# Two output-column blocks of the first branch's gates: five pairs of k-tiles instead of four by seven products, all four weight sums read from DRAM

## The chip, the cores and the metric

One core of a Trainium2 chip runs the whole program. The metric is device time in microseconds (us), the median of several executions. Three executions of the kernel before took 1547.37, 1547.99 and 1548.03 us, so the median is 1547.99 us. A profiled execution of the same kernel is what all rows below come from; its own time was 1548.36 us.

## The reference

The program is one layer of a decoder trunk for 256 positions of width 2048, all in float32:

```python
h = rms_norm(x, norm_mix_pre[l]);  proj = h @ w_in[l]
a_in, b_in, q, kv, nsa_g, merge_g = jnp.split(proj, splits, axis=-1)
y_a, y_b, y_c = conformer_conv(a_in, ...), chunked_spatial_gating(b_in, ...), native_sparse_attention(q, kv, nsa_g, ...)
g_a, g_b, g_c = jnp.split(jax.nn.sigmoid(merge_g), 3, axis=-1)
x = x + rms_norm((g_a * y_a + g_b * y_b + g_c * y_c) @ w_o[l], norm_mix_post[l])
h = rms_norm(x, norm_ffn_pre[l]);  u = causal_dwconv3(h @ w_up[l]);  u_g, u_v = jnp.split(u, 2, axis=-1)
x = x + rms_norm((silu(u_g) * u_v) @ w_down[l], norm_ffn_post[l])
```

The change touches the product `h @ w_in` for `merge_g`, and in it the 2048 columns of `g_A`, the gates of the first branch.

## The kernel before

**Products.** TensorE works on float32 values that are split in two: a high part of fewer bits (`hi`, copied by ScalarE) and the rest (`lo`, subtracted by VectorE). One product of a 128x128 tile by 128x512 weights is three matmuls: high by high, high by rest, rest by high. Each block of weights thus goes through a load into one of five buffers `wraw` (queued on SyncE, "SP" in the profile), a copy on ScalarE (ACT) into one of four buffers `whi`, and a subtraction on VectorE (DVE) into one of four buffers `wlo`.

**Sevens.** A gate block is 256 positions by 1024 columns, over 16 k-tiles. Two halves of positions by two halves of columns by two k-tiles are a 2x2 by 2x2 product of blocks: eight block products, 24 matmuls, when done plainly (`k_tiles`), or seven, 21 matmuls, by Winograd's form of Strassen's method (`Seven.seven`). The seven need four sums of weight blocks and some sums of activations (`sh`, `s3`, made for five pairs while attention runs, in `input_sums`). Seven's products go to four main accumulators `c` and four side accumulators `p1`, `p5`, `p6`, `p7`; `combine` adds the sides up at the end, and `totals` adds the main ones and takes the tanh. In a `seven`, SP loads the blocks `b` and half of `r` from the weights, and sums from DRAM: `a` (two sums, into one of two buffers `qa`), one more into the other half of `r`, and, if four sums are in DRAM, the fourth into `tt`. If only three are there, VectorE adds the fourth into `tt` itself. ScalarE and VectorE then split `b`, `a`, `r` and `t` (a half block).

**The sums in DRAM.** GpSimd (POOL) issues DMAs that build the weight sums in DRAM tiles `ahead`, long before they are used: a copy of blocks, then DMAs that add other blocks to them. `ahead_steps` yields these steps in a fixed order: gate blocks 0 to 3, the output projection ("o"), then the 33 pairs of the down projection. `ahead_by(mark, n)` issues the next `n` of them when a given result of the main work exists: POOL first copies one column of it into `tick`, which makes it wait. POOL runs in order, one DMA after the other, each waiting for those that it adds to. Steps that are left at the end of the first half are spread over the 44 iterations of the up projection.

**Order of the work.** First the projections of the branches, the convolution and the attention's inputs; then `branch()` (gates and output of the second branch, column block `cb` 0 to 3) and `outs_a()` (output of the first) with attention in between as background work; then the gate blocks `gates_7(0)` and `gates_7(1)` (first branch), `gates_7(2)` and `gates_7(3)` (third branch, with its output projection), the output projection "o", the up projection, the down projection in two column halves ("pair 0" and "pair 1"). Gate block `i` begins with `lead` plain k-tiles, then come `len(GP[i])` sevens with `between[j]` plain tiles ahead of seven `j`, then the remaining plain tiles. `then()` is emitted after the lead tiles: for block 0 it lets attention finish, for block 1 it takes the totals of block 0 and multiplies the gates into the sum (`gate_a`). Matmuls of these blocks are chained in the order in which they are written (`in_line`), so are the splits on ACT and DVE (`fixed`); the rest is ordered by a scheduler. Names in the rows: `g03b` is block `b` of gate block 0, seven 3; `pg` main, `pg0s` side accumulators; `Ct<-O` the last step of attention.

Of the kernel before, what the change touches and what calls it, by code (L numbers as in the profile page):

```python
# [23 lines left out]
F32 = mybir.dt.float32  # L24
# [10 lines left out]
NFT = FF // 128  # L35
# [8 lines left out]
NEXT = ((6, 4, 5, 0), (1, 2))  # L44
SUMS = [[2 + (n % 2 or n >= 16) for n in range(len(TURNS[0]))], [3 + (n % 2 == 0) for n in range(len(TURNS[1]))]]

GP = [[0, 1, 2, 3]] * 3 + [[0, 1, 2, 3, 4]]
GREST = [list(range(2 * len(gp), KT)) for gp in GP]
OP, OREST = [0, 1, 2, 4], [6, 7, *range(10, KT)]
BA, BB, BC, BG, RUSH, SUMS_AT = 2100, 2200, 2200, 6500, 1.0, 3  # L50
PR = 1000
# [14 lines left out]
def block(ctx: ExitStack, tc: tile.TileContext, x, xf, x0, fp, cst, rows, sgw, w1, w2, wf_a, wt_bv, wf_bu, wf_c,  # L66
# [58 lines left out]
    def pooled(op, *args, **kw):  # L125

        with ExitStack() as order:
            for ins in in_pool:
                order.enter_context(tc.issue_after(ins))
            in_pool[:] = [op(*args, **kw).ins]  # L130

    tick = PZ.tile([128, 1], F32, name="tick")
    made = {}

    def ahead_steps():

        quads = [(("g", cp, j), (wt_gq[cp, j] if cp < 3 else wt_cq[j]), 3) for cp in range(4) for j in range(len(GP[cp]))]
        quads += [(("o", j), wt_oq[j], 3) for j in range(len(OP))]
        quads += [((p, j), (wt_dq0, wt_dq1)[p][n], SUMS[p][n]) for p in range(2) for n, j in enumerate(TURNS[p])]
        add = {"accum_op": ALU.add}  # L140
        late = []
        for i, (key, src, sums) in enumerate(quads):
            dst = DR.tile([128, sums, 512], F32, name=f"ahead{i}")
            made[key] = dst, sums
            src = src.rearrange("p (b n) -> p b n", b=4)
            yield dst[:, 0:2], src[:, 2:4], {}
            if late:
                yield late.pop(0)
            if sums > 2:
                yield dst[:, 2:], src[:, 4 - sums:2], {}  # L150
            yield from late
            yield dst[:, 0:2], src[:, 1:3], add
            late = [(dst[:, x], dst[:, y], add) for x, y in ((sums - 1, 1), (2, 3))[:sums - 2]]
        yield from late

    steps = list(ahead_steps())

    def ahead_by(mark, n):

        pooled(G.tensor_copy, tick, mark)  # L160
        for dst, src, how in steps[:n]:
            pooled(G.dma_start, dst, src, **how)
        del steps[:n]

    def split2(raw):
# [1027 lines left out]
    def branch():  # L1193

        for cb in range(4):
            pg = [PS.tile([128, 512], F32, tag="acc", name=f"pg0{cb}{t}") for t in range(2)]
            for q in range(4):
                hs = granule(wt_g[cb * 4 + q])
                for k, ts_ in in_order(q):
                    hi, lo = hs[(k % 4) // 2]  # L1200
                    c = slice((k % 2) * 512, (k % 2) * 512 + 512)
                    for t in ts_:
                        ts = slice(t * 128, t * 128 + 128)
                        with ExitStack() as order:
                            if (cb, k) == (1, 0):
                                order.enter_context(tc.issue_after(norm["v"]))
                            mm_t(pg[t], hT[:, k, 0, ts], hT[:, k, 1, ts], hi[:, c], lo[:, c], k == 0, k == KT - 1)
                if (cb, q) == (0, 2):
                    until("m")
                    debt[0] = 0.0  # L1210
                elif q < 3:
                    if (cb, q) == (1, 2):
                        marks.add("outputs")
                    pump(BUDGET)
            tgs = {}
            for t in range(2):
                for a in range(2):
                    tgs[t, a] = q1(f"mg0{cb}{t}{a}")
                    with tc.high_priority(offset=int(PR)):
                        gated[0] = S.activation(tgs[t, a], pg[t][:, a * 256:a * 256 + 256], AF.Tanh,  # L1220
                                                scale=rh[:, t:t + 1]).ins
            marks.add("gates")
            pump(BUDGET)
            py = [PS.tile([128, 512], F32, tag="acc", name=f"py0{cb}{t}") for t in range(2)]
            for q in range(2):
                hs = granule(wt_p[cb * 2 + q])
                if cb == 0 and q == 0:
                    until("B")
                act = Bt_box["t"]
                for k, ts_ in in_order(q):  # L1230
                    hi, lo = hs[(k % 4) // 2]
                    c = slice((k % 2) * 512, (k % 2) * 512 + 512)
                    for t in ts_:
                        ts = slice(t * 128, t * 128 + 128)
                        with ExitStack() as order:
                            if (cb, k) == (0, 7):
                                until("v")
                                debt[0] = max(debt[0], 0.0)
                                order.enter_context(tc.issue_after(norm["v"]))
                            pe_last[0] = mm_t(py[t], act[:, k, 0, ts], act[:, k, 1, ts], hi[:, c], lo[:, c], k == 0, k == 7)  # L1240
                if q == 0:
                    pump(BUDGET)
            for t in range(2):
                for a in range(2):
                    cc = slice(cb * 512 + a * 256, cb * 512 + a * 256 + 256)
                    y = mac[:, t, cc]
                    with tc.high_priority(offset=int(PR)):
                        V.scalar_tensor_tensor(y, tgs[t, a], 1.0, py[t][:, a * 256:a * 256 + 256], op0=ALU.add,
                                               op1=ALU.mult)
            ahead_by(mac[:, 0, cb * 512:cb * 512 + 1], (4, 8, 12, 8)[cb])  # L1250
            pump(BUDGET)

    def outs_a():

        for cb in range(4):
# [14 lines left out]
                with tc.high_priority(offset=int(PR)):  # L1270
                    V.tensor_copy(ya[:, t, cb * 512:cb * 512 + 512], py[t])
            if cb < 3:
                ahead_by(ya[:, 0, cb * 512:cb * 512 + 1], (8, 4, 0)[cb])
            pump(BUDGET)

    def m_sums(n):
# [69 lines left out]
    def gates_7(i, between, lead=2, then=None):  # L1346
# [4 lines left out]
        def begin():  # L1351
            if then:
                then()
            pr.p1, pr.p5, pr.p6, pr.p7 = four(i, "s")
            gates_of.append(s8([128, 2, 2, 512], F32, f"gates{i}"))
        in_sevens(pr, wt_gp[i] if i < 3 else wt_cp, wt_gq[i] if i < 3 else wt_cq, GREST[i], between, hx, g_acts, ("g", i), lambda j: box["qa"][:, j % 2],
                  lambda: box["tt"], f"g{i}", lead, begin)
        return pr

# [11 lines left out]
        return then  # L1371

    prs = []
    prs.append(gates_7(0, (0, 0, 0, 0), 6, attended))
    prs.append(gates_7(1, (1, 0, 0, 0), 4, gated_a(0)))
    for cp in range(2):
        pr = gates_7(2 + cp, (0,0,0,0,0) if cp else (1,0,0,0), 3 if cp else 4, None if cp else gated_a(1))
        gates = gates_of[2 + cp]
# [271 lines left out]
    for i in range(NFT):  # L1650
# [19 lines left out]
        for j, (k0, k1) in enumerate(PAIRS):  # L1670
            if i == k0:
                first = acc[0]
            elif i == k1:
# [8 lines left out]
                    pooled(G.dma_start, extra[j], apart_.bitcast(F32))  # L1682
                if j < AWAY:
                    pooled(G.dma_start, away[j], dst.rearrange("p x a b -> p x (a b)").bitcast(F32))
        ahead_by(g2(i, slice(0, 1))[0].bitcast(F32), max(0, len(steps) - count * (NFT - 2 - i) // (NFT - 2)))
    P2b_ctx.close()


# [235 lines left out]
def _layout(inp):  # L1924
# [92 lines left out]
                c(np.concatenate([w[k1, 0], w[k1, 1], w[k0, 1], w[k0, 0]], axis=2)))  # L2017

    sevens = [by_sevens(w_in[:, g_cols[2048 + 1024 * i:3072 + 1024 * i]], GP[i], GREST[i]) for i in range(4)]
    wt_gp, wt_gq = (np.stack(a) for a in zip(*sevens[:3]))  # L2020
    wt_cp, wt_cq = sevens[3]
    wt_op, wt_oq = by_sevens(g["w_o"][0][:, 0:1024], OP, OREST)

    xf = c(g["x"].reshape(T, KT, 128).transpose(2, 1, 0))
# [26 lines left out]
```

## Time and profile before

| | |
|---|---|
| median of the timed runs | 1547.99 us (1547.37 to 1548.03) |
| the profiled execution, its own time | 1548.36 us |
| span from its first to its last instruction | 1546.7 us |
| TensorE busy | 1538.8 us, 99% of the span |
| VectorE, ScalarE, GpSimd busy | 86%, 62%, 15% |
| granted TensorE clock | 1.00 throughout |
| gate blocks of the first branch | 528 us (first matmul of block 0) to 613 us (end of block 1) |

In a row of a group of instructions, the count is followed by the busy time and the mean duration of one, and then by the idle time of the engine just before them and what ended it. Durations of matmuls overlap, since they are pipelined: the pace is read from a run of matmuls without a break in the chain of waits (time of the run over their number). A timeline row has start, duration, engine, line, operation, tiles and, in brackets, the idle time before it. A windows row gives for one stretch the busy time of each engine, the granted clock, the mean busy share of the 16 DMA engines and the bytes moved. "SPq" is the queue of DMAs on SyncE.

### The profile page before, as it was taken

How to read it: one execution, taken by the hardware profiler on the slowest of the kernel's cores; microseconds unless marked ns; L12 is line 12 of the kernel's file. 1: busy time of each engine (PE TensorE's matmuls, PEld its weight loads, DVE VectorE, ACT ScalarE, POOL GpSimd, SP SyncE). 2: the span in 40 equal slices, each digit the busy share in tenths (PEclk: the TensorE clock that was granted, in tenths of full speed). 3: DMA queues.
4: the chain of work that ended last, by engine and by line, in shares of the span. 5: the costliest groups of instructions: out<-in, count | busy, mean ns of one | idle time of the engine just before them, and what ended most of it. 6: DMA issues, size and time to landing. Idle time of an engine off the chain costs nothing.

```text
span 1546.7 us, 23457 instructions
## 1 busy us (share of the span) xinstructions
PE 1538.8 (99%) x8138; PEld 1313.3 (85%) x8138; DVE 1336.8 (86%) x2282; ACT 961.5 (62%) x1509; POOL 229.8 (15%) x350
## 2 busy tenths in 40 slices
PE   9999999999999999999999999999999999999998
PEld 8888889888877788888888888888888888888887
DVE  7899999978778689979878888888888888899898
ACT  7645544456776766656666666666565656576774
POOL 1021460211121100000000122222222221100000
PEclk9999999999999999999999999999999999999999
DMA  9598997998889877767884699999999999989895
GB/s 372 189 299 266 293 295 224 271 289 270 251 243 266 257 241 267 254 221 262 270 268 160 207 307 332 316 324 295 292 280 288 279 292 285 324 283 344 315 380 207
DMA packets 131512, 428.24 MB, mean 277 GB/s; under 512 B 15104, under 2 KB 16880, under 8 KB 130624
## 3 DMA queue, kind: packets, MB, share of 16 engines
q1 hardware_dynamic: 99936, 329.99, 60.8%
q0 software_dynamic: 30880, 96.09, 26.2%
q8 instruction: 64, 1.05, 0.3%
q10 hardware_dynamic: 576, 0.66, 0.1%
q14 instruction: 56, 0.46, 0.1%
HBM read 418.55 MB, written 92.01 MB: 330 GB/s over the span
## 4 chain that ended last, share of the span: by engine, by line
PE 95%; issue 2%; DVE 2%; DMA 1%; ACT 0%; POOL 0%; DVEq 0%; POOLq 0%
PE ps L229 29%; PE ps L236 15%; PE pg L1096 8%; PE pd1a L1096 4%; PE pd0b L1096 4%; PE pd0a L1096 3%; PE pd1b L1096 3%; PE py L250 3%; PE py L251 3%; PE py L252 3%; PE poa L1096 2%; PE pg L251 1%; PE pg L252 1%; PE pg L250 1%; PE po L252 1%
## 5 line engine op out<-in xcount | busy, mean ns | idle before, releaser
L200 ACT ACTIVATE whi<-wraw 128x1024 fp32r<-128x1024 f32 (+1 forms) x344 | 361.1, 1055 | 205.5 <-PE ps L229 115.0
L201 DVE TENSOR_TENSOR wlo<-wraw,whi 128x1024 fp32r<-128x1024 f32 (+1 forms) x344 | 419.1, 1224 | 72.7 <-ACT whi L200 54.1
L229 PE MATMUL ps<-h2T,whi 128*128 128x512 f32 x1360 | 317.2, 390 | 0.0
L229 PEld LDWEIGHTS ps<-h2T,whi 128*128 128x128 f32 x1360 | 252.4, 188 | 50.4
L236 PEld LDWEIGHTS ps<-h2T,wlo 128*128 128x128 f32 x1360 | 169.4, 192 | 3.6
L236 PE MATMUL ps<-h2T,wlo 128*128 128x256 f32 x1360 | 170.7, 283 | 0.0
L229 PE MATMUL ps<-hT,whi 128*128 128x512 f32 x640 | 151.7, 390 | 0.0
L229 PEld LDWEIGHTS ps<-hT,whi 128*128 128x128 f32 x640 | 118.0, 188 | 23.0
L1052 DVE TENSOR_TENSOR wlowraw<-wraw,whiwraw 128x1024 fp32r<-128x1024 f32 x72 | 87.1, 1222 | 25.7 <-ACT whiwraw L1052 23.6
L558 DVE SCALAR_TENSOR_TENSOR cv<-hb,fps,cv 128x256 f32<-128x256 f32 x240 | 107.0, 502 | 0.1
L1052 ACT ACTIVATE whiwraw<-wraw 128x1024 fp32r<-128x1024 f32 x72 | 75.6, 1057 | 38.6 <-PE py L252 10.1
L1660 ACT ACTIVATE fa<-fs,fps 128x256 f32<-128x256 f32 x88 | 52.7, 598 | 53.6 <-DVE fs L275 51.7
L236 PEld LDWEIGHTS ps<-hT,wlo 128*128 128x128 f32 x640 | 80.8, 191 | 2.6 <-DVE wlo L201 0.3
L236 PE MATMUL ps<-hT,wlo 128*128 128x256 f32 x640 | 82.3, 283 | 0.1
L130 POOL DMA_DIRECT2D ahead<-ahead x54 | 44.3, 821 | 241.8 <-DMA ahead<-in_wt_dq_dram 104.0
L130 POOL DMA_DIRECT2D ahead<-in_wt_dq_dram x91 | 69.4, 879 | 71.5 <-DMA ahead<-in_wt_dq_dram 70.4
L272 ACT ACTIVATE t<-ps 128x256 f32<-128x256 f32 x125 | 47.5, 381 | 49.5 <-PE ps L236 26.5
L1096 PE MATMUL pg<-whiwraw,hT 128*128 128x512 f32 x240 | 75.5, 390 | 0.0
L130 POOL COPY tick<-gh 128x1 f32<-128x1 f32 x44 | 35.1, 799 | 192.0 <-ACT gh L1668 192.0
L1661 DVE SCALAR_TENSOR_TENSOR fa<-fs,fps,fa 128x255 f32<-128x255 f32 x88 | 42.4, 481 | 16.6 <-ACT fa L1660 16.5
L1096 PEld LDWEIGHTS pg<-whiwraw,hT 128*128 128x128 f32 x240 | 45.0, 188 | 10.1 <-issue 0.8
L273 DVE TENSOR_TENSOR t<-ps,t 128x256 f32<-128x256 f32 x125 | 52.7, 424 | 0.5 <-ACT t L272 0.5
(2568 smaller groups left out, 3345.8 us busy)
## 6 DMA issues: line engine op xcount, KB each, us to landing
wraw<-in_wf_up_dram SPq DMA_DIRECT2D x176, 512.0 KB, 6.9
ahead<-in_wt_dq_dram POOLq DMA_DIRECT2D x74, 512.0 KB, 10.1
wraw<-in_wt_p_dram SPq DMA_DIRECT2D x48, 512.0 KB, 6.4
wraw<-in_wt_dq_dram SPq DMA_DIRECT2D x33, 512.0 KB, 5.7
wraw<-in_wf_a_dram SPq DMA_DIRECT2D x32, 512.0 KB, 5.6
wraw<-in_wt_g_dram SPq DMA_DIRECT2D x32, 512.0 KB, 6.3
fin<-ahead SPq DMA_DIRECT2D x32, 512.0 KB, 5.8
ahead<-ahead POOLq DMA_DIRECT2D x54, 256.0 KB, 6.8
```

The source lines that it names most:

```text
L130: in_pool[:] = [op(*args, **kw).ins]
L200: S.activation(hi[:, :n], raw[:, :n], AF.Copy)
L201: V.tensor_sub(lo[:, :n], raw[:, :n], hi[:, :n].bitcast(F32))
L229: ins = PE.matmul(ps, lhsT=ws[k // 8][0][:, c:c + 128], rhs=mov[:, k], start=bool(k == 0 and first), stop=bool(k == n - 1 and not first), ...
L236: ins = PE.matmul(ps[:, 1], lhsT=ws[k // 8][1][:, c:c + 128], rhs=mov[:, k, 0], start=bool(k == 0 and not first), stop=bool(k == n - 1 and ...
L250: PE.matmul(ps, lhsT=xh, rhs=hi, start=first, stop=False)
L251: PE.matmul(ps, lhsT=xh, rhs=lo, start=False, stop=False)
L252: return PE.matmul(ps, lhsT=xl, rhs=hi, start=False, stop=last).ins
L273: V.tensor_add(t1 if rb is not None else dst, ps[:, 0], t1)
L558: V.scalar_tensor_tensor(ca[:, j], hb[:, j, k:k + T], w(j, k), ca[:, j], op0=ALU.mult, op1=ALU.add)
L1052: seq[eng] = [op(*args, **kw).ins]
L1096: ins = PE.matmul(bank, lhsT=a[x], rhs=w[y], start=first and j == 0, stop=bool(last and j == 2), skip_group_check=more).ins
```

## The change

Gate blocks 0 and 1 take five pairs by sevens (k-tiles 0 to 9) where they took four, and six k-tiles stay plain where eight were. All four sums of their ten pairs come from DRAM; the steps that build them are therefore five per pair, not four. Block 0 has four lead tiles where it had six, block 1 no plain tile between the lead and the first seven where it had one; both keep two plain tiles at the end (block 1 had three). Before the up projection, an addition of two blocks is issued as two DMAs with rows of 2 KB where it was one DMA with rows of 4 KB. The numbers of steps at three of the places are raised (10 for 8, 8 for 4, 2 for 0).

```diff
-GP = [[0, 1, 2, 3]] * 3 + [[0, 1, 2, 3, 4]]
+GP = [list(range(n)) for n in (5, 5, 4, 5)]
 GREST = [list(range(2 * len(gp), KT)) for gp in GP]
+GSUMS = (4, 4, 3, 3)
...
+    def gates_in(cp):
+        group = len(GP[cp]) - 4
+        n = sum(len(GP[i]) - 4 == group for i in range(cp))
+        return ((wt_gp, wt_gq), (wt_cp, wt_cq))[group][0][n], ((wt_gp, wt_gq), (wt_cp, wt_cq))[group][1][n]
...
-        quads = [(("g", cp, j), (wt_gq[cp, j] if cp < 3 else wt_cq[j]), 3) for cp in range(4) for j in range(len(GP[cp]))]
+        quads = [(("g", cp, j), gates_in(cp)[1][j], GSUMS[cp]) for cp in range(4) for j in range(len(GP[cp]))]
...
-    def ahead_by(mark, n):
+    def ahead_by(mark, n, up=False):
 
         pooled(G.tensor_copy, tick, mark)
         for dst, src, how in steps[:n]:
-            pooled(G.dma_start, dst, src, **how)
+            if how and not up and len(dst.shape) > 2:
+                for b in range(dst.shape[1]):
+                    pooled(G.dma_start, dst[:, b], src[:, b], **how)
+            else:
+                pooled(G.dma_start, dst, src, **how)
         del steps[:n]
...
-            ahead_by(mac[:, 0, cb * 512:cb * 512 + 1], (4, 8, 12, 8)[cb])
+            ahead_by(mac[:, 0, cb * 512:cb * 512 + 1], (4, 10, 12, 8)[cb])
...
-                ahead_by(ya[:, 0, cb * 512:cb * 512 + 1], (8, 4, 0)[cb])
+                ahead_by(ya[:, 0, cb * 512:cb * 512 + 1], (8, 8, 2)[cb])
...
-    prs.append(gates_7(0, (0, 0, 0, 0), 6, attended))
-    prs.append(gates_7(1, (1, 0, 0, 0), 4, gated_a(0)))
+    prs.append(gates_7(0, (0, 0, 0, 0, 0), 4, attended))
+    prs.append(gates_7(1, (0, 0, 0, 0, 0), 4, gated_a(0)))
...
-        ahead_by(g2(i, slice(0, 1))[0].bitcast(F32), max(0, len(steps) - count * (NFT - 2 - i) // (NFT - 2)))
+        ahead_by(g2(i, slice(0, 1))[0].bitcast(F32), max(0, len(steps) - count * (NFT - 2 - i) // (NFT - 2)), True)
```

The remaining lines of the diff group the weights of blocks with five pairs (`wt_cp`, `wt_cq`) and with four (`wt_gp`, `wt_gq`).

**ACT at the start of gate block 0**, in the kernel before (`whiwraw` are splits of plain tiles, `ep` and `Ct` attention's last steps):

```order
L938 ACTIVATE ep_5061<-pp_5333 128x512
L938 ACTIVATE ep_5061<-pp_5334 128x512
L1052 ACTIVATE whiwraw_5748_5750<-wraw_5748 128x1024
L1052 ACTIVATE whiwraw_5766_5768<-wraw_5766 128x1024
L1052 ACTIVATE whig00b<-wraw_5791 128x1024
L954 ACTIVATE Ct<-O_5332 128x4x128
L1052 ACTIVATE whig00a<-qa 128x1024
L1052 ACTIVATE whig00r<-wraw_5794 128x1024
L1052 ACTIVATE whig00t<-tt 128x512
```

and in the changed one:

```order
L948 ACTIVATE ep_5083<-pp_5357 128x512
L948 ACTIVATE ep_5083<-pp_5358 128x512
L1062 ACTIVATE whig00b<-wraw_5790 128x1024
L1062 ACTIVATE whig00a<-qa 128x1024
L1062 ACTIVATE whig00r<-wraw_5793 128x1024
L964 ACTIVATE Ct<-O_5356 128x4x128
L1062 ACTIVATE whig00t<-tt 128x512
```

Two plain tiles are gone from between attention's last steps and the first seven, so the first seven's `b`, `a` and `r` now stand ahead of `Ct`.

**DVE at the start of gate block 1**, before (`gates<-pg` totals of block 0, L1336 and L1337 the multiplication of the gates into the sum, `wlo` the splits):

```order
L1337 TENSOR_TENSOR mac<-mac,gates_5790 128x512
L1052 TENSOR_TENSOR wlowraw_6105_6108<-wraw_6105,whiwraw_6105_6107 128x1024
L1337 TENSOR_TENSOR mac<-mac,gates_5790 128x512
L1052 TENSOR_TENSOR wlog10b<-wraw_6123,whig10b 128x1024
L1052 TENSOR_TENSOR tt<-wraw_6123,wraw_6126 128x512
L1337 TENSOR_TENSOR mac<-mac,gates_5790 128x512
L1052 TENSOR_TENSOR wlog10a<-qa,whig10a 128x1024
L1052 TENSOR_TENSOR wlog10r<-wraw_6126,whig10r 128x1024
L1052 TENSOR_TENSOR wlog10t<-tt,whig10t 128x512
```

and in the changed kernel:

```order
L1347 TENSOR_TENSOR mac<-mac,gates_5789 128x512
L1062 TENSOR_TENSOR wlog10b<-wraw_6148,whig10b 128x1024
L1347 TENSOR_TENSOR mac<-mac,gates_5789 128x512
L1062 TENSOR_TENSOR wlog10a<-qa,whig10a 128x1024
L1347 TENSOR_TENSOR mac<-mac,gates_5789 128x512
L1062 TENSOR_TENSOR wlog10r<-wraw_6151,whig10r 128x1024
L1062 TENSOR_TENSOR wlog10t<-tt,whig10t 128x512
```

One plain tile's split and the addition into `tt` are gone; the work on the gates of block 0 stays ahead of the splits of the first seven.

**SP in gate block 0, sevens 2 and 3**, in the changed kernel (`in_wt_cq` the weights, `ahead` the sums in DRAM):

```order
L1121 DMA qa<-ahead_69 128x1024
L119 DMA wraw_5922<-in_wt_cq_dram 128x1024
L1130 DMA tt<-ahead_69 128x512
L119 DMA wraw_5925<-in_wt_cq_dram 128x512
L1126 DMA wraw_5925<-ahead_70 128x512
L1121 DMA qa<-ahead_70 128x1024
L119 DMA wraw_5966<-in_wt_cq_dram 128x1024
L1130 DMA tt<-ahead_70 128x512
```

The loads of `tt` are new; the others stood in the same order before.

More of the change, by code (lines that the diff above doesn't have):

```diff
@@ L1355, in begin @@
             gates_of.append(s8([128, 2, 2, 512], F32, f"gates{i}"))
-        in_sevens(pr, wt_gp[i] if i < 3 else wt_cp, wt_gq[i] if i < 3 else wt_cq, GREST[i], between, hx, g_acts, ("g", i), lambda j: box["qa"][:, j % 2],
+        in_sevens(pr, *gates_in(i), GREST[i], between, hx, g_acts, ("g", i), lambda j: box["qa"][:, j % 2],
                   lambda: box["tt"], f"g{i}", lead, begin)
@@ L2019, in _layout @@
     sevens = [by_sevens(w_in[:, g_cols[2048 + 1024 * i:3072 + 1024 * i]], GP[i], GREST[i]) for i in range(4)]
-    wt_gp, wt_gq = (np.stack(a) for a in zip(*sevens[:3]))
-    wt_cp, wt_cq = sevens[3]
+    wt_gp, wt_gq = (np.stack(a) for a in zip(*[x for x, gp in zip(sevens, GP) if len(gp) == 4]))
+    wt_cp, wt_cq = (np.stack(a) for a in zip(*[x for x, gp in zip(sevens, GP) if len(gp) == 5]))
     wt_op, wt_oq = by_sevens(g["w_o"][0][:, 0:1024], OP, OREST)
```

## The prediction

> **What bounds the kernel now.** I read the page's busy times first, then the chain of waits, then what TensorE waits for, and then stretches of time for the stages that the change touches.
>
> ```profile
> PE 1538.8 (99%) x8138; PEld 1313.3 (85%) x8138; DVE 1336.8 (86%) x2282; ACT 961.5 (62%) x1509; POOL 229.8 (15%) x350
> PE 95%; issue 2%; DVE 2%; DMA 1%; ACT 0%; POOL 0%; DVEq 0%; POOLq 0%
> ```
>
> TensorE (PE) is busy for 1538.8 of 1546.7 us, and the chain that ends last is PE for 95%. So only two things can move the end: the number of matmuls, and a load or a split that comes late enough to stop them. The gate blocks run as one unbroken piece:
>
> ```profile
> 549.83 2.73 PE pg0s L1096 x12
> 566.90 21.09 PE pg L1096 x93
> 587.99 2.73 PE pg1s L1096 x12
> ```
>
> The last two rows are the chain of waits from the last seven of block 0 across its end into block 1: 93 matmuls in 21.09 us, 0.2268 us each, with nothing between. At that pace a seven (21 matmuls) takes 4.76 us, a plain tile (12) 2.72 us.
>
> **What the change removes.** In each of two blocks a pair of k-tiles goes from 24 matmuls to 21. That is 2 x 3 = 6 matmuls, 6 x 0.2268 = **1.36 us** of PE. VectorE also gets lighter:
>
> ```profile
> L1052 DVE TENSOR_TENSOR wlowraw<-wraw,whiwraw 128x1024 fp32r<-128x1024 f32 x9 | 10.8, 1223 | 0.6 <-ACT whiwraw L1052 0.2
> L1052 DVE TENSOR_TENSOR tt<-wraw,wraw 128x512 f32<-128x512 f32 x7 | 4.8, 685 | 0.0
> ```
>
> A seven costs it three splits of 1.22, half a one of 0.69 and the addition of 0.69, 5.03 us against PE's 4.76; with the fourth sum from DRAM it is 4.35. Eight additions go (5.5 us); two pairs become sevens at 4.35 instead of two splits of 1.22 (3.8 us more). I credit nothing for either: PE does not wait for VectorE in these blocks, so the cover is PE's own unbroken work.
>
> **What it adds in the two blocks: bytes.** A seven loads `b`, `a` and `r` (512 KB each), 1.573 MB, and now `tt` as well (256 KB): 1.835 MB per 4.76 us, 385 GB/s for five sevens on end, where 330 were needed. The trace has stretches of such work:
>
> ```profile
> 842.00:1317.00 475.00, 475.00 (x2745) 420.92 (x2744) 410.26 (x723) 296.35 (x477) 105.78 (x158) 1.00 0.95 290
> 1322.00:1430.00 108.00, 108.00 (x477) 88.98 (x476) 100.55 (x113) 74.03 (x81) 6.56 (x11) 1.00 0.95 323
> 548.30:567.40 19.10, 19.10 (x85) 15.77 (x84) 16.76 (x18) 14.33 (x16) 0.00 (x0) 1.00 0.73 243
> 1445.00:1515.00 70.00, 70.00 (x310) 57.85 (x309) 64.81 (x64) 53.50 (x58) 0.54 (x1) 1.00 1.01 374
> 1450.98 4.76 PE pd1a L1096 x21
> ```
>
> The columns are the stretch, its length, busy time (and instructions) of PE, PEld, DVE, ACT and POOL, the clock, the DMA share and GB/s. The fourth row is the nearest: sevens of the down projection, half of them with four sums, 374 GB/s for 70 us with the DMA engines full, PE busy throughout, and a seven still in 4.76 us (last row). The second (323 GB/s) has POOL's additions beside it; in the sevens of block 0 (third row) POOL does nothing, and the DMA share of 0.73 leaves room. At a rate r, one seven is short by 1.835/r - 4.76 us: 0.15 at 374, 0.92 at 323. Five of them: 0.7 or 4.6 us per block, of which some 2 us are absorbed by loads sent ahead (two `qa`, five `wraw`; my estimate: 7.35 us from the free buffer to its use against
>
> ```profile
> qa<-ahead SPq DMA_DIRECT2D x17, 512.0 KB, 5.1
> ```
>
> 5.1 us to landing). So the cost is 0 at 374 and 2.6 us per block, 5.2 in both, at 323. I take **0**, by the nearest row; the plain tiles on both sides need only 0.524 MB per 2.72 us and refill the buffers.
>
> The Trainium skill, "DMA: Bandwidth & Descriptors", section "Where 436 GB/s comes from", speaks against the change: it puts transfers between HBM and SBUF at about 358 GB/s for a core. By it a seven would need 1.835 MB / 358 = 5.13 us, 0.36 too many, 3.6 us for ten, less what was sent ahead; the row of 374 GB/s lies above that figure, so the sum does not use it.
>
> **The hand-over into block 0.** Two lead tiles fewer: the first sevens' splits come 5.44 us of PE nearer to attention's end, and attention's last steps now stand behind three splits on ACT.
>
> ```profile
> 540.76 0.60 ACT L954 ACTIVATE Ct<-O 128x512 fp32r<-128x512 f32 x1 [1.50 <-PE O L859]
> 541.39 0.69 DVE L955 TENSOR_TENSOR Ct<-O,Ct 128x512 fp32r<-128x512 f32 x1 [0.27 <-ACT Ct L954]
> 551.23 1.06 ACT L1052 ACTIVATE whig01a<-qa 128x1024 fp32r<-128x1024 f32 x1 [0.26 <-PE pg0s L1096]
> ```
>
> ACT was waiting for `O` (1.50 us idle), so the splits ahead of it fit. The lead tiles keep PE until 549.83 - 5.44 = 544.4; `Ct` is done at 542.1, and the first seven's `b`, `a`, `r` stand in the buffers' turns that two plain tiles and `b` had. Margin 2.3 us: cost 0; if `Ct` slips by as much as one split on each engine (1.06 + 1.22), still 0.
>
> **The hand-over into block 1.** One plain tile less (2.72 us) stands ahead of the first seven, while VectorE does the totals and `mac` without a gap:
>
> ```profile
> 581.30 1.22 DVE L1052 TENSOR_TENSOR wlowraw<-wraw,whiwraw 128x1024 fp32r<-128x1024 f32 x1
> 584.17 0.69 DVE L1052 TENSOR_TENSOR tt<-wraw,wraw 128x512 f32<-128x512 f32 x1
> 585.38 1.22 DVE L1052 TENSOR_TENSOR wlog10a<-qa,whig10a 128x1024 fp32r<-128x1024 f32 x1
> 586.51 1.22 DVE L1052 TENSOR_TENSOR wlog10r<-wraw,whig10r 128x1024 fp32r<-128x1024 f32 x1
> 587.65 0.69 DVE L1052 TENSOR_TENSOR wlog10t<-tt,whig10t 128x512 fp32r<-128x512 f32 x1
> ```
>
> The first two rows leave the stretch, so `a` ends at 586.6 - 1.9 = 584.7 less a little where rows overlap (584.3 by starts); `t` at 588.3 - 1.9 = 586.4. The seven now starts at 587.99 - 2.72 = 585.27, and uses its factors one after the other, `t` some 2.6 us in. Margins are 0.5 to 1.5 us. Bounds: 0 to 1.5 us; I take 0. At the end of block 1, two plain tiles (5.44 us) cover the sides' `combine` where three did; block 0 ended with two before, and its piece of 93 has no gap.
>
> **The sums in DRAM.** Two additions more per gate quad and the split of additions lengthen POOL's row. What waits for its steps:
>
> ```profile
> ahead<-ahead POOLq DMA_DIRECT2D x54, 256.0 KB, 6.8
> 170.10 0.82 POOL L130 DMA_DIRECT2D ahead<-ahead  x1 [5.00 <-DMA ahead<-in_wt_gq_dram]
> 209.65 0.82 POOL L130 DMA_DIRECT2D ahead<-ahead  x1 [3.70 <-DMA ahead<-in_wt_gq_dram]
> L130 POOL COPY tick<-ub x8: 456/2306/5073, 163.6 to 210.7; 128x1 f32<-128x1 f32 x8
> L641 DVE TENSOR_TENSOR ub<-ub,sgf x8: 465/467/467, 211.6 to 223.6; 128x256 f32<-128x256 f32 x8
> 517.95 1.12 POOL L130 COPY tick<-ya 128x1 f32<-128x1 f32 x1
> ```
>
> From the second to the third row are three quads: 13.2 us each, for four steps. The fifth step adds at worst a whole 6.8 us: 20.0 for five, 4.0 a step instead of 3.3, and over the 16 steps of this phase 11 us; I estimate about 2, since the copy of the next quad overlaps it. That puts the last `tick<-ub`, at 210.7, 2 to 11 us later; VectorE writes over `ub` until 223.6, so the eight in-place products have 12.9 us before the last of them is held. POOL's last steps ahead of the blocks move from 518 to about 530, with the quads used first built first. Cost **0**.
>
> In the up projection ten more steps (118 for 108) move ten x 0.524 MB: at the first windows row's 290 GB/s 18 us of DMA time, spread over 475 us. Who would wait is ACT, for weights; it waits for PE instead:
>
> ```profile
> ACT whi L200 <- PE ps L229: 115.0, 110, 4.1
> POOL tick L130 <- ACT gh L1668: 192.0, 24, 31.6
> ```
>
> 115.0 us of slack there against 18: cost **0**; without that cover up to 18 us. POOL itself idles 192.0 us for its marks.
>
> **One stall that may move.** PE's largest single wait for a split is at 395 us:
>
> ```profile
> PE pg L251 <- DVE wlo L201: 1.3, 1, 1.3
> 387.27 1.06 ACT L200 ACTIVATE whi<-wraw 128x1024 fp32r<-128x1024 f32 x1 [3.86 <-DMA wraw<-in_wt_g_dram]
> 396.99 0.50 PE L251 MATMUL pg<-wlo,hT 128*128 128x512 f32 x1 [1.27 <-DVE wlo L201]
> ```
>
> A weight load landed late while POOL's DMAs of `cb` 1 ran; these are now ten steps and narrower. Bounds: -1.3 us (gone) to about +1.5 us (as much again, here or at another `cb`). I take 0, that is, it stays.
>
> **The sum.** -1.36 + 0 + 0 + 0 + 0: the span goes from 1546.7 to 1545.3, the profiled execution from 1548.36 to 1547.0. The median of the timed runs is 0.37 us below the profiled one: 1547.99 - 1.36 = **1546.6 us**.
>
> **The rivals.** *The late weight goes or doubles.* For it: POOL's burst is reordered just there; against: only one such wait in 8138 matmuls. Without it 1546.6 - 1.3 = 1545.3; with a second one of 1.5 us, 1548.1.
>
> *DMA sets the pace of the sevens* (the other side). In blocks 0 and 1 every seven needs 385 GB/s. It decides where the rate falls below some 355 GB/s (the prefetch's 2 us used up: 1.835 x 5 / (23.8 + 2)); at 346 the 1.36 us are eaten, at 323 the two blocks lose 5.2 us: 1546.6 + 5.2 = 1551.8. The skill's figure from above would give up to 1546.6 + 3.6 = 1550.2, as an estimate. For it: 323 GB/s stands in a row; against: POOL's additions are in that row, and 374 is the nearer.
>
> *VectorE is late into block 1.* Price up to 1.5 us, 1548.1, if the totals or the `mac` products start later by a microsecond than I read; against it: VectorE loses 1.9 us there and PE's lead shrinks by 2.7, a net of 0.8 against margins of 0.5 to 1.5.
>
> *POOL's longer row delays something earlier or the up projection.* If a fifth of the up stage's 18 us shows, +3.6: 1550.2; the whole, 1564. For it: the DMA share of 0.95 in that stretch; against it: ACT's slack of 115.0 us.
>
> *The fifth pair saves nothing*, because PE was paced by something else in these blocks: 1548.0. The pieces without a break speak against it.
>
> **How the numbers follow.** About 0.2%, 3.1 us, is what a measurement can tell from no change here, so 1544.9 to 1551.1 counts as the same. Forecast 0.57; the stall gone 0.12, doubled 0.10; DMA's pace 0.07; VectorE late 0.05; POOL or the up projection 0.06; nothing saved 0.03. Nearly all of these lie within 3.1 us. Faster than that needs the stall's loss and 0.4 us more: 0.06. Slower needs the whole of DMA's price or more than a fifth of the up stage's: 0.11, with what I have not seen. The same: 0.83. The likeliest alone reaches from 1545.6 to 1548.2; with the stall's lower end and half of the DMA cases the range is 1544.9 to 1550.0.
>
> **What would show it right or wrong.** In the changed kernel's chain, block 0 to block 2 should be PE without a break, with six matmuls fewer in the whole. Wrong by the DMA rival: gaps of PE ahead of `pg` or `pg0s`, with ACT waiting for `qa`, `tt` or `wraw` from DMA, and a window of the sevens at a DMA share of 1.0 below 360 GB/s. Wrong at block 1: a PE wait for `wlog10b` to `wlog10t`. Wrong on POOL: VectorE's `ub` products waiting for `tick`, or ACT's `whi` waiting for `wraw<-in_wf_up`. The stall at 395 is read from PE's waits for `wlo`.

## The result: slower, through a wait at 235 us

The changed kernel took 1556.78 us (median of 13 executions, 1549.04 to 1559.53); the kernel before 1547.99 us. The ratio is 1.0051, 95% interval 1.0039 to 1.0062. The forecast was 1546.6 us, with 1544.9 to 1550.0 as its range. The profiled execution took 1558.58 us, its span is 1555.9 us against 1546.7: 9.2 us to explain.

The page of the changed kernel, busy times and the chain by engine:

```profile
PE 1539.5 (99%) x8132; PEld 1313.5 (84%) x8132; DVE 1336.6 (86%) x2278; ACT 963.4 (62%) x1513; POOL 238.5 (15%) x393
PE 86%; DMA 9%; issue 2%; DVE 1%; POOL 1%; ACT 0%; DVEq 0%; POOLq 0%; ACTq 0%; SPq 0%
```

Six matmuls are gone (8132 for 8138), but in the chain that ends last, PE's share fell from 95% to 86%, and DMA's rose from 1% to 9%. What PE and VectorE waited for (total us, times, longest):

```profile
PE ps L246 <- DVE wlo L211: 9.2, 1, 9.2
DVE ub L651 <- POOL tick L131: 9.2, 2, 7.7
```

Neither row has a counterpart before. They belong together, in the timeline of VectorE, PE and POOL in the projections at 184 to 237 us:

```profile
183.97 0.81 POOL L131 DMA_DIRECT2D ahead<-ahead  x1 [11.03 <-DMA ahead<-in_wt_cq_dram]
192.21 0.80 POOL L131 DMA_DIRECT2D ahead<-ahead  x1 [6.66 <-DMA ahead<-ahead]
206.10 0.81 POOL L131 DMA_DIRECT2D ahead<-ahead  x1 [10.59 <-DMA ahead<-in_wt_cq_dram]
...
226.93 0.43 DVE L651 TENSOR_TENSOR ub<-ub,sgf 128x256 f32<-128x256 f32 x1 [1.46 <-POOL tick L131]
235.10 0.43 DVE L651 TENSOR_TENSOR ub<-ub,sgf 128x256 f32<-128x256 f32 x1 [7.74 <-POOL tick L131]
235.78 1.22 DVE L211 TENSOR_TENSOR wlo<-wraw,whi 128x1024 fp32r<-128x1024 f32 x1
...
237.05 2.07 PE L246 MATMUL ps<-hT,wlo 128*128 128x256 f32 x8 [9.23 <-DVE wlo L211]
```

VectorE multiplies `sgf` into `ub` in place. POOL's copies `tick<-ub` read `ub`, so the write must wait for the copy; behind the write, on VectorE, stands the split `wlo` of the next weights, and behind that PE. The copies are 23 us later than before (210.7). A quad's five steps now hold two serial waits, 11 us for the copies and 6.7 us for the addition before; how much of the lateness that explains is settled by experiments further down:

```profile
L131 POOL COPY tick<-ub x8: 418/1160/2858, 171.7 to 234.0; 128x1 f32<-128x1 f32 x8
```

The windows around the stop (stretch, length, busy us of PE, PEld, DVE, ACT and POOL, granted clock, DMA share, GB/s) show a second price:

```profile
226.00:237.00 11.00, 1.82 (x15) 1.57 (x14) 2.32 (x5) 2.56 (x6) 4.06 (x8) 0.81 0.66 160
237.00:243.00 6.00, 5.95 (x18) 5.08 (x19) 6.00 (x14) 0.37 (x1) 0.15 (x1) 0.50 1.06 237
243.00:260.00 17.00, 17.00 (x121) 16.71 (x121) 17.00 (x35) 9.30 (x14) 8.90 (x17) 1.00 0.97 269
```

The clock was already halved during the last 4 us of the stop (the first row's 0.81 over 11 us), and after it PE's granted clock is 0.50 for 6 us more: matmuls cost twice their time, 2.85 us lost (summed from the starts of successive matmuls against those of like matmuls elsewhere). The Trainium skill, "TensorE: Matmul & The Clock Gate", section "Part 1: The HAM clock gate", says that TensorE runs at half clock after an idle window of some 3.4 us and returns after about as long a busy one; the trace agrees with the half, and here the half lasted some 6 us after the stop.

The gate blocks did what was forecast. The chain through both, and on into block 2:

```profile
576.58 18.37 PE pg L1106 x81
594.94 2.73 PE pg1s L1106 x12
616.79 21.09 PE pg L1106 x93
```

There is no break, at 0.2268 us a matmul, and the window over the sevens of block 1 has the DMA engines nearly full with PE busy throughout:

```profile
594.00:617.00 23.00, 23.00 (x103) 18.98 (x102) 20.96 (x21) 17.42 (x20) 0.00 (x0) 1.00 0.97 351
```

To see where time goes, take the start of the same matmul in two traces and watch the difference grow. The columns are the changes, in us against the trace of the kernel before, from one landmark to the next: the start of the program up to the first projection (50 us); up to the last matmul of `pvs` (259 us); up to the last `O` (540 us); gate blocks 0 and 1; output, third branch and the up projection (to 1321 us); pair 0 of the down projection; and the end. The other rows are the experiments of the next section, where each is named by the label in the first column.

| kernel | start | to `pvs` | to `O` | gate blocks | to down | pair 0 | end | span |
|---|---|---|---|---|---|---|---|---|
| changed | +0.21 | **+11.92** | -1.84 | **-1.28** | 0.00 | **+0.99** | -0.72 | +9.28 |
| e1_sgf | +1.98 | +1.66 | -1.84 | -1.28 | -0.02 | +1.99 | -0.71 | +1.78 |
| e2_whole | +2.01 | +2.37 | -1.84 | -1.28 | -0.03 | +1.38 | -0.75 | +1.86 |
| e3_split_only | -0.43 | +0.76 | -1.13 | -0.01 | -0.02 | -0.09 | -0.37 | -1.29 |
| e4_three_sums | -0.23 | +0.76 | -1.86 | -1.12 | -0.18 | +0.23 | -0.61 | -3.01 |
| f1_early_steps | +0.26 | +3.30 | -1.84 | +15.61 | 0.00 | -0.03 | -0.74 | +16.56 |
| f2_three_whole | -0.30 | 0.00 | -0.34 | -1.14 | -0.16 | 0.00 | -0.60 | -2.54 |
| f3_late_pool | -0.27 | +13.69 | -0.51 | 0.00 | -0.02 | +0.13 | +0.13 | +13.15 |
| f4_three_whole_sgf | +1.81 | +0.13 | -0.90 | -1.11 | -0.17 | -0.05 | -0.60 | -0.89 |
| g2_four_early | +0.38 | +0.86 | +4.10 | +2.53 | -0.01 | -0.01 | -0.75 | +7.10 |
| g3_more_in_up | +0.04 | -0.03 | -1.04 | -1.14 | -0.18 | +1.55 | -0.61 | -1.41 |

The start differs by up to 2 us between executions, in a stretch where no edit changed anything, so a single span is not a verdict; the stages are. Of the changed kernel: 11.9 lost at `ub`, 1.8 gained in the stall at 395 us and its neighbourhood, 1.28 gained in the gate blocks, 0.99 lost in pair 0, 0.7 gained at the very end (not looked into).

Of the thirteen executions ten ran at a mean clock of 0.996 to 0.998 and took 1554.6 us or more, and three at 0.999 to 1.000 took 1549.0 to 1550.1, so these three probably had no stop long enough to lower the clock, which is not shown, since only an execution with it was traced.

### The profile page after: what moved, and what is told of

Same layout as the page of the kernel before. It is cut to its first block, busy times and chain, and to the rows that moved or that the text cites. A ratio compares the mean times of both kernels' runs of the same rounds, so it can differ in the third digit from the quotient of the medians.

```text
span 1555.9 us, 23556 instructions
## 1 busy us (share of the span) xinstructions
PE 1539.5 (99%) x8132; PEld 1313.5 (84%) x8132; DVE 1336.6 (86%) x2278; ACT 963.4 (62%) x1513; POOL 238.5 (15%) x393
## 4 chain that ended last, share of the span: by engine, by line
PE 86%; DMA 9%; issue 2%; DVE 1%; POOL 1%; ACT 0%; DVEq 0%; POOLq 0%; ACTq 0%; SPq 0%
PE ps L239 23%; PE ps L246 12%; PE pg L1106 7%; DMA ahead<-in_wt_cq_dram 5%; PE pd1a L1106 4%; PE py L260 3%; PE pd0b L1106 3%; PE py L261 3%; PE py L262 3%; PE pd1b L1106 3%; PE pd0a L1106 3%; DMA ahead<-ahead 3%; PE poa L1106 2%; PE pg L261 2%; PE pg L260 2%
## 5 line engine op out<-in xcount | busy, mean ns | idle before, releaser
L131 POOL DMA_DIRECT2D ahead<-ahead x66 | 55.4, 839 | 490.2 <-DMA ahead<-in_wt_dq_dram 171.3
L1062 DVE TENSOR_TENSOR wlowraw<-wraw,whiwraw 128x1024 fp32r<-128x1024 f32 x68 | 82.1, 1222 | 20.2 <-ACT whiwraw L1062 18.4
L1062 ACT ACTIVATE whiwraw<-wraw 128x1024 fp32r<-128x1024 f32 x68 | 71.2, 1057 | 34.8 <-PE py L262 10.1
L246 PEld LDWEIGHTS ps<-hT,wlo 128*128 128x128 f32 x640 | 81.9, 193 | 11.9 <-DVE wlo L211 9.5
L1106 PE MATMUL pg<-whiwraw,hT 128*128 128x512 f32 x208 | 65.7, 391 | 0.0
L131 POOL DMA_DIRECT2D ahead<-in_wt_cq_dram x60 | 48.6, 1085 | 10.5 <-DMA ahead<-in_wt_cq_dram 9.8
L262 PE MATMUL pg<-whi,hT 128*128 128x512 f32 x128 | 50.2, 393 | 0.0
```

Of the source, the lines that this page charges most:

```text
L246: ins = PE.matmul(ps[:, 1], lhsT=ws[k // 8][1][:, c:c + 128], rhs=mov[:, k, 0], start=bool(k == 0 and not first), stop=bool(k == n - 1 and ...
L262: return PE.matmul(ps, lhsT=xl, rhs=hi, start=False, stop=last).ins
L1062: seq[eng] = [op(*args, **kw).ins]
L1106: ins = PE.matmul(bank, lhsT=a[x], rhs=w[y], start=first and j == 0, stop=bool(last and j == 2), skip_group_check=more).ins
```

## Experiments

Theory T is what the rows above suggest: POOL's row is late, and PE's loss comes through VectorE's write over `ub`. T-sum and T-split name what makes the row late; T2, further down, is on the up projection.

**Is it the wait for `tick`?** The product is written into `sgf`, so that a late copy of `ub` holds up nobody.

```diff
-        V.tensor_mul(u, u, f.rearrange("p a t -> p (a t)"))
+        f = f.rearrange("p a t -> p (a t)")
+        V.tensor_mul(f, u, f)
+        u = f
```

> The eight products ub * sgf are written into sgf instead of over ub; nothing else is changed. POOL's copies tick<-ub then hold up nobody, however late they are. Theory T (POOL's row is late, VectorE's write over ub waits for the last tick<-ub, PE waits for the splits queued behind it): the wait of 9.2 us and the lower clock after it (2.9 us) go, the last tick<-ub stays near 234 us, and the time is 1546.5 us (1545.5 to 1548). Rival R (the loads of weights themselves come late there, because POOL's DMAs take the bandwidth): PE still stands still between 220 and 245 us for at least 5 us, and the time stays above 1553 us.

Measured (`e1_sgf`): 1548.29 us, ratio to before 1.0001 (0.9991 to 1.001). POOL is as late as in the changed kernel, but PE's long wait is gone. The rows of the copies and of the products, and then some of PE's waits in this run:

```profile
L131 POOL COPY tick<-ub x8: 467/1204/2855, 173.7 to 237.0; 128x1 f32<-128x1 f32 x8
L652 DVE TENSOR_TENSOR sgf<-ub,sgf x8: 409/412/415, 214.5 to 228.0; 128x256 f32<-128x256 f32 x8
```

```profile
PE pvs L261 <- DVE wlo L211: 0.9, 1, 0.9
PE pd0a L1108 <- DVE wloq_12a L1064: 0.8, 1, 0.8
PE pd0a L1108 <- ACT whiq_12a L1064: 0.7, 1, 0.7
```

The last product is at 228.0 us when nothing holds it; the start of this execution was 2.0 us late, so in the changed kernel's time it is due at some 226, and stood there until 235.1. R is out, as it was put (5 us or more). But 1546.5 was expected and the time is that of the kernel before: 1.99 us are lost in pair 0 of the down projection (the last two rows are 1.5 of them). So there is a second loss. A smaller one stays in the first stretch, 1.66 us up to `pvs`: PE still waits for late splits there, 0.9 us in the first row of waits and 0.3 us in another, though no copy holds VectorE up. Why they are late was not followed.

**The same wait in the kernel before.** If theory T is right, four sums and split additions are not needed for it: a late POOL is enough.

```diff
-        ahead_by(ub[:, j, 0:1], 2)
+        ahead_by(ub[:, j, 0:1], 3)
...
-        ahead_by(qf[:, i, 0:1], 2)
+        ahead_by(qf[:, i, 0:1], 1)
```

> The kernel before with three instead of two of POOL's steps at each mark of ub, and one instead of two at each mark of qf: nothing but POOL's row is later there (seven more steps of 3.3 us ahead of the last tick<-ub, 211 + 23 = 234 us). Gates, sums and additions are those of the kernel before. T: VectorE waits some 9 us for tick, PE stands still about as long, the granted clock falls for 5 to 10 us after it (2 to 3 us more); 1557 to 1560 us. Rival (the wait needs the four sums or the split additions, by their load on the DMA engines): no wait of PE over 2 us there, 1548 to 1550 us.

Measured (`f3_late_pool`): 1562.42 us, ratio 1.01 (1.0084 to 1.0115). The waits of PE and VectorE, POOL's copies, and the window after the stop:

```profile
PE ps L236 <- DVE wlo L201: 10.9, 1, 10.9
DVE ub L641 <- POOL tick L130: 12.2, 2, 9.0
```

```profile
L130 POOL COPY tick<-ub x8: 467/692/1508, 163.3 to 234.8; 128x1 f32<-128x1 f32 x8
```

```profile
239.00:246.00 7.00, 7.00 (x37) 6.35 (x36) 7.00 (x17) 1.83 (x3) 1.81 (x4) 0.87 0.95 286
```

The last copy came at 234.8 where 234 was worked out, and the old kernel shows the whole mechanism by itself, some 2 us dearer than expected. The clock came back sooner than the 5 to 10 us expected: 0.87 over 7 us is 1.8 us at half, and PE had gone on at 236.97, so the half lasted 3.9 us after the stop. T stands.

**What makes POOL late: the fourth sum or the splitting?** Three runs: the changed kernel with whole additions; the kernel before with split ones; the changed kernel with three sums (`GSUMS = (3, 3, 3, 3)`, VectorE adds the fourth).

```diff
-            if how and not up and len(dst.shape) > 2:
+            if False:
```

> Additions of two blocks are issued whole again, as one DMA with rows of 4 KB; the five pairs and the four sums stay. Theory T-split (the narrower, doubled DMAs make POOL's row slow): the last tick<-ub comes before 216 us, VectorE does not wait for it, and the time is 1546 to 1548 us. Theory T-sum (the second serial addition of a quad with four sums makes it slow): the last tick<-ub comes at 225 to 232 us, the wait is 3 to 8 us, the time 1551 to 1556 us.

> The kernel before (four pairs, three sums), with nothing but the splitting of its additions into two DMAs with rows of 2 KB ahead of the up projection. T-split: the last tick<-ub moves from 211 us to 225 or later, VectorE waits for it, the time is 1553 us or more. T-sum: it stays below 220 us, no wait, 1548.0 us plus or minus 1.5.

> The changed kernel with three sums in DRAM for all gate blocks: VectorE adds the fourth for blocks 0 and 1 again, POOL has four steps a quad, additions stay split, and 108 steps are left for the up projection as before the change. T-sum: last tick<-ub below 220 us, no wait of VectorE for it, POOL done with the up projection's steps before the down projection begins; 1546.6 us (1545.5 to 1548.5). T-split: it comes at 225 us or later and the time is 1553 us or more. If VectorE's 5.03 us a seven against PE's 4.76 binds over five sevens, up to 2 us more in the two blocks.

Measured: 1548.79 us (`e2_whole`, ratio 1.0002, 0.9993 to 1.0011), 1547.13 us (`e3_split_only`, 0.9993, 0.9984 to 1.0002) and 1546.49 us (`e4_three_sums`, 0.9989, 0.9979 to 0.9998), with 1548.24 us for the kernel before timed beside them. The rows of `tick<-ub`, in the same order:

```profile
L131 POOL COPY tick<-ub x8: 520/924/2542, 168.9 to 227.6; 128x1 f32<-128x1 f32 x8
```

```profile
L130 POOL COPY tick<-ub x8: 466/786/4306, 163.2 to 215.5; 128x1 f32<-128x1 f32 x8
```

```profile
L131 POOL COPY tick<-ub x8: 470/856/4390, 163.4 to 215.8; 128x1 f32<-128x1 f32 x8
```

Against 210.7 before: the fourth sum alone makes the last copy 16.9 us later (about 15 without the late start of that execution), splitting alone 4.8, both 23.3. T-sum had the right tick (225 to 232 forecast, 227.6 found) and the wrong price: it expected 3 to 8 us of waiting, and that run fitted by a hair, since its last products came at 228.2 to 228.6 us with no wait for `tick`. Only the two together go past the edge, which is why T-sum's time for the first run failed; in the other two runs it held in tick and time, and T-split failed in all three. The stretch up to `pvs` has smaller losses beside these: 0.76 us where split additions stand beside three sums, next to nothing where additions are whole and sums three (0.00, 0.13 and -0.03 in runs further down), but 0.86 to 3.30 us in the four runs with four sums, split or whole, in which nothing waits for `tick`. Why was not followed. VectorE's fourth sum, priced at up to 2 us, cost the run with three sums 0.16 us in the gate blocks (-1.12 for -1.28).

**The second loss.** With 118 steps left for the up projection, POOL no longer finishes in it. Rows of its copies `tick<-gh`, first before, then in the changed kernel with POOL's wait for them and one of its last additions, then with `sgf`; in the changed kernel all the stages there stand 9.0 us later, so 1349 is 1340 in the old kernel's time:

```profile
L130 POOL COPY tick<-gh x44: 282/782/1807, 868.9 to 1330.5; 128x1 f32<-128x1 f32 x44
```

```profile
L131 POOL COPY tick<-gh x44: 279/657/2357, 877.9 to 1349.1; 128x1 f32<-128x1 f32 x44
```

```profile
POOL tick L131 <- ACT gh L1678: 31.6, 1, 31.6
```

```profile
1348.62 0.81 POOL L131 DMA_DIRECT2D ahead<-ahead  x1 [9.38 <-issue]
```

```profile
L131 POOL COPY tick<-gh x44: 282/655/2357, 869.4 to 1343.5; 128x1 f32<-128x1 f32 x44
```

POOL's wait for its marks, 192.0 us in 24 pieces before, is 31.6 in one: it was always behind. To test it from both sides, ten steps were moved out of the up projection in the version with four sums and `sgf`, and ten into it in the version with three whole sums (first and second hunk).

```diff
-                ahead_by(ya[:, 0, cb * 512:cb * 512 + 1], (8, 8, 2)[cb])
+                ahead_by(ya[:, 0, cb * 512:cb * 512 + 1], (8, 8, 12)[cb])
...
-                ahead_by(ya[:, 0, cb * 512:cb * 512 + 1], (8, 8, 2)[cb])
+                ahead_by(ya[:, 0, cb * 512:cb * 512 + 1], (8, 0, 0)[cb])
```

> As the run with sgf (products written into sgf, all else as changed), and ten more of POOL's steps are issued at the last mark of ya (12 for 2), so that 108 are left for the up projection, as before the change. Theory T2 (in the up projection POOL cannot do 118 steps in time; its last ones run into the first half of the down projection and make a weight or a sum late there): POOL's last tick<-gh comes back from 1343 to about 1330 us, the 2.0 us that PE lost in pair 0 of the down projection fall to 0.3 or less, 1546.5 us (1545.5 to 1548). Rival R2 (pair 0 loses for another reason, the sevens' own loads): the loss stays 1 us or more, 1548.3 us. And if the DMA rate bounds the sevens of gate block 0 once POOL's additions run beside them (385 GB/s needed), PE loses 1 to 4 us between 545 and 575 us: 1548 to 1551 us.

> Five pairs, three sums, whole additions, and ten steps fewer at the last two marks of ya (0 and 0 for 8 and 2), so that 118 are left for the up projection, as in the changed kernel, of quads with three sums only. T2 (118 steps are more than POOL can do there): POOL's last tick<-gh comes at 1335 us or later where it came at 1329, and pair 0 of the down projection loses 0.5 to 2 us; 1547.3 us (1546.3 to 1548.5). Rival R3 (118 steps fit, and it was POOL's lateness at the up projection's start that ran on): the last tick<-gh at 1331 or earlier, no loss, 1546.1 us.

Measured with 108 steps left (`f1_early_steps`): 1560.87 us (1.0089, 1.0075 to 1.0103); with 118 (`g3_more_in_up`): 1547.60 us (0.9999, 0.999 to 1.0008), where the same kernel with 108 takes 1546.07 (`f2_three_whole`, further down). Pair 0 follows the number of steps: with 118 it loses 0.99, 1.99, 1.38 and 1.55 us, with 108 between -0.09 and +0.23, whether sums are three or four. T2 stands for the number of steps; its tick was put at 1335 or later, and 1333.5 was already enough. By which load or split the last steps delay pair 0 was not followed: PE's losses there come in pieces of a quarter to one us, at splits of different blocks in each trace.

```profile
L131 POOL COPY tick<-gh x44: 283/739/2382, 866.6 to 1333.5; 128x1 f32<-128x1 f32 x44
```

The first of the two runs brought what its last sentence had priced at 1 to 4 us, at 15.6. The twelve steps at the last mark of `ya` ran on POOL beside the sevens. The window of gate block 0, the one after it, and what ACT waited for between 556 and 606 us:

```profile
545.00:581.00 36.00, 33.60 (x133) 26.31 (x132) 24.07 (x24) 19.39 (x22) 8.47 (x13) 0.91 1.04 328
581.00:605.00 24.00, 18.06 (x60) 12.68 (x59) 16.03 (x20) 10.51 (x13) 0.83 (x2) 0.86 0.76 238
```

```profile
ACT whiwraw L1064 <- DMA wraw<-in_wt_cp_dram: 11.8, 4, 3.5
ACT whig04a L1064 <- DMA qa<-ahead: 3.1, 1, 3.1
```

The 328 GB/s are all that moved. Parted by queue for the same window 545 to 581 us (packets, MB, share of the time of the 16 DMA engines; the hardware queue has SP's loads, the software queue POOL's DMAs), with the time from issue to landing of six weight loads:

```profile
q1 hardware_dynamic: 2902, 8.31, 63.2%
q0 software_dynamic: 1401, 3.46, 40.2%
wraw<-in_wt_cp_dram SPq DMA_DIRECT2D x6, 512.0 KB, 15.1
```

The loads get 8.31 MB in 36 us, 231 GB/s, and land after 15.1 us where those of `wraw` in the window of block 1 of the changed kernel took 5.3 to 6.2; POOL's copies and additions take 40% of the engines' time for 29% of the bytes. At that rate a seven's 1.835 MB take 7.9 us against PE's 4.76, and PE waits, with the clock below 1 again. So the prediction's DMA rival is real; in the changed kernel it is only held off by POOL being nearly done before the sevens (its last issues are at 545 to 548 us, the first seven's side products begin at 554.5).

**Can the ten steps go elsewhere?** With four sums, `sgf` and whole additions they were spread over earlier marks.

```diff
-            ahead_by(mac[:, 0, cb * 512:cb * 512 + 1], (4, 10, 12, 8)[cb])
+            ahead_by(mac[:, 0, cb * 512:cb * 512 + 1], (6, 14, 16, 8)[cb])
```

> Five pairs with four sums from DRAM, products into sgf, additions whole, and ten steps moved from the up projection to three earlier marks of mac (6, 14 and 16 for 4, 10 and 12), so that POOL is done ahead of gate block 0 and 108 steps are left for the up projection. T and T2 together: no wait for tick, no loss in pair 0 of the down projection (0.3 us or less), the gate blocks give 1.28 us: 1546.2 us (1545.2 to 1547.5), no better than three sums. Rival (denser additions beside the branches' products make weights late there): PE loses 1 to 3 us more between 340 and 500 us, 1547.5 to 1549.5.

Measured (`g2_four_early`): 1554.28 us (1.0045, 1.0029 to 1.0062). The rival was right, and still too low:

```profile
PE zp L723 <- ACT whi L210: 3.5, 1, 3.5
PE pg0s L1108 <- ACT whig03a L1064: 0.9, 1, 0.9
PE pg0s L1108 <- DVE wlog03a L1064: 0.8, 1, 0.8
```

```profile
362.00:367.00 5.00, 4.62 (x15) 3.76 (x16) 3.67 (x3) 4.12 (x6) 0.00 (x0) 0.66 0.80 270
```

A weight came 3.5 us late at 362 us (with a lowered clock behind it), and POOL still ran into gate block 0, where 2.5 us were lost. No place tried for these ten steps was free: 1.0 to 2.0 us in the up projection's overrun; at `mac` 5.9 us up to `O` and 3.8 in the gate blocks (4.10 and 2.53 where the changed kernel has -1.84 and -1.28); at `ya` 16.9 in the gate blocks.

**Five pairs without what makes POOL late.** Three sums and whole additions: the fifth pairs, the shorter leads and the numbers of steps are all that is left of the change; and the same with `sgf`.

> Five pairs in blocks 0 and 1, three sums in DRAM, additions whole: of the change only the fifth pairs, the shorter leads and the numbers of steps. T: POOL's row as in the kernel before, last tick<-ub at 211 to 214 us, no wait for it; the gate blocks give their 1.1 to 1.3 us; 1546.6 us (1545.6 to 1547.6), as with three sums and split additions (1546.5) or up to 0.7 us less. Rival (the split additions were what took the late weight at 395 us away, 1.3 us): that stall is back, 1547.8 us.

> As the run before the last (five pairs, three sums, whole additions), and the products of ub and sgf go into sgf. T: the last waits behind tick are gone too, PE's waits for wlo between 210 and 245 us are below 0.3 us; 1546.0 us (1545.2 to 1547.2), the fastest so far. Rival (no wait for tick was left to take away): the same as with the products over ub, within 0.3 us.

Measured: 1546.07 us (`f2_three_whole`, ratio 0.999, 0.9981 to 0.9999) and 1546.03 us (`f4_three_whole_sgf`, 0.9989, 0.998 to 0.9997): 1.8 to 1.9 us below the kernel before timed beside them (1547.91), about 0.1%, with the upper ends of the intervals close to 1. `sgf` adds nothing, since no copy is late. The late weight at 395 us is back nearly whole in the first (1.2 us where it was 1.3; 0.6 in the second), so its rival was right about the stall, and wrong about the time, which came below the forecast all the same:

```profile
PE pg L261 <- DVE wlo L211: 1.2, 1, 1.2
```

```profile
L131 POOL COPY tick<-ub x8: 224/695/3277, 163.3 to 210.1; 128x1 f32<-128x1 f32 x8
```

With `e4_three_sums`, which is as far below its own reference (1.75 us), these are the best versions found, and a little faster than both kernels; whether additions are split makes no difference to the time here. All three keep VectorE's additions, which cost next to nothing: -1.14, -1.11 and -1.12 us in the gate blocks, against -1.28 with the fourth sum from DRAM. The window of block 1's sevens with three sums (split additions) suggests why it is not quite nothing, VectorE being busy for 23.92 of 24.00 us:

```profile
580.00:604.00 24.00, 24.00 (x106) 19.54 (x105) 23.92 (x28) 16.91 (x19) 0.00 (x0) 1.00 0.83 279
```

## Why the prediction was wrong, point by point

**The six matmuls: right.** 1.36 us forecast, 1.28 measured in the gate blocks.

**VectorE worth nothing there: nearly right.** The fourth sum from DRAM saves 0.15 us in ten sevens.

**Bytes at no cost: right as long as POOL rests.** No seven was late, at 351 GB/s in the window of block 1. The figure of 358 GB/s from "DMA: Bandwidth & Descriptors" in the Trainium skill, section "Where 436 GB/s comes from", by which ten sevens would have lost up to 3.6 us, did not show as a loss; the window of 351 lies below it and cannot tell, the prediction's row of 374 lies above it (364 of them loads, 25.49 MB in 70 us). The price of the DMA rival was worked out wrongly: 323 GB/s was read as a rate to which POOL holds the loads, but PE never waited in that row, so it shows what was asked for and no bound, and it counts POOL's own bytes (3.55 of 34.85 MB, most of them loads of `home`, with a single addition issued). With POOL's copies and additions beside them the loads got 231 GB/s. In the prediction's own sum that is 3.2 us short for a seven and 15.9 for the five of block 0, less the 2 us sent ahead, as an estimate; the gate blocks took 15.6 us more than before, where 5.2 had been priced for two blocks. The late loads also delayed VectorE's work on the gates, and PE's clock fell; the parts were not separated.

**Both hand-overs: right.** Margins of 0.5 to 2.3 us were enough.

**The sums in DRAM, cost 0: the step that failed.** It named the place, the in-place products on `ub` behind the last `tick<-ub`, and gave 12.9 us before they are held and at most 11 us of lateness. The first was about right: the product was due at 226, 15 us after the old copy. The lateness was 23.3 us. Two terms were mis-sized. (1) Only the 16 steps at `ub` were counted. The 24 steps at `hb` before them were late as well: the first `tick<-ub` moved from 163.6 to 171.7 us, 8.1 us. Their cover, POOL's waits for `hb`, was used up but for the wait for the first mark (33.3 us now):

```profile
POOL tick L130 <- DVE hb L622: 74.2, 7, 33.5
```

```profile
POOL tick L131 <- DVE hb L632: 34.5, 2, 33.3
```

(2) A step was priced at 4.0 us at worst, one serial addition of 6.8 us more a quad. From the first copy to the last there are 14 steps: 47.1 us before, 3.4 each, and 62.3 now, 4.5 each. The splitting was given no price, and is worth 4.8 us over the whole by itself. And since 9.2 us of standing still also halved the clock, the bill was 11.9 us, not 9.2.

**The up projection, cost 0: right for the stage, wrong behind it.** No matmul of it was late. But 192.0 us of POOL waiting for marks were read as room for ten steps more. POOL's steps end on landings of some 10 us (10.1 for a 512 KB copy before), one after the other. Among the kernels with three sums and whole additions, ten steps more took POOL's waits from 118.8 us (`f2_three_whole`) to 31.6 (`g3_more_in_up`), at least 8.7 us a step; in the changed kernel all but the first wait was gone too, and the rest ran into pair 0, for 0.99 us (1.0 to 2.0 in four traces). The rival "POOL's longer row" had both places in its name, a chance of 0.06, and a price for the wrong one.

**The late weight at 395 us: went,** as its rival had it; the stretch to `O` gained 1.84 us. That stretch varies between -0.34 and -1.86 us among the kernels with five pairs, apart from the one with denser steps at `mac`, and is -1.13 and -0.51 in the two with four pairs, so the fifth pairs are not needed for it; which of POOL's transfers move it was not separated.

**Slower at 0.11** came from cases that each seemed covered. The cover had been read as a sum of idle time, not followed step by step along POOL's row.

## What to carry to other kernels

A copy that only paces a queue still reads its tile, and whoever overwrites that tile waits for the queue: mark with something that is not written again, or leave the queue ample slack at that place. A row of DMAs, each waiting for the one before, has a length of its own (landings, not bytes or issue time); if it grows, walk along it from its first step to the last reader, across every mark, since idle time at marks is used up once. And when a sum can be made by an engine that has the time, as VectorE had here, that is cheaper than a DMA in a busy stretch.

## What the runs showed of the hardware beyond what was expected

A wait of TensorE of several us costs more than its length: after 9.2 us of standing still the granted clock was 0.50 for some 6 us more (2.85 us lost), after 10.9 us of it for 3.9 us more, and after 3.5 us of it, at 362 us, it was 0.66 on the mean of the next 5 us. Copies and additions in DRAM beside loads took 40% of the DMA engines' time for 29% of the bytes and held the loads to 231 GB/s (328 in all, at a DMA share of 1.04), where a stretch almost without them moved 374 at 1.01. Issuing an addition of two blocks as two DMAs of half the size made POOL's row 4.8 us longer up to its last `tick<-ub`. With three sums the stretch to `O` was shorter with split additions (-1.86 us against -0.34 to -1.04 with whole ones), but whole additions with four sums reached -1.84 as well, so that a gain from the splitting is not shown.
